# Row normalisation by the absolute sum, fp32: another division of the scaling between VectorE and ScalarE, and one row sum moved in the first tile

## Chip, cores, metric

One core of one Trainium2 chip. The metric is the device time of the whole program in microseconds (us) on that core. A change counts as faster or slower from 2% on.

## The reference

```python
x = np.random.randn(32, 512, 1024).astype(np.float32)

def reference(x):
    sums = np.sum(np.abs(x), axis=-1, keepdims=True)
    return (x / (sums + 1e-8)).astype(np.float32)
```

That is 16384 rows of 1024 elements, 67.1 MB in and 67.1 MB out, with little arithmetic for each byte.

## The kernel before

The rows go through on-chip memory in eleven tiles: ten with 12 rows per partition (128 x 12 x 1024 fp32, 6.29 MB) and a last one with 8 (4.19 MB). There are four tile buffers. SyncE issues the loads, ScalarE's queue the stores, and a load waits until the store that last used its buffer has landed. VectorE forms the sums and reciprocals of a tile and scales most of its rows in place; ScalarE scales the others at the same time.

```python
    R = 12
    BUFS = 4
    HEAD = 32
    ...
    rows = [R] * ((per_partition - HEAD) // R + 2) + [HEAD - 2 * R]   # 10 x 12, then 8
    ...
    def normalize(x_tile, r0, k, kv):          # k rows, VectorE scales the first kv
        s = stats.tile([P, R], FP32)
        nc.vector.tensor_reduce(out=s[:, :k], in_=x_tile[:, r0 : r0 + k, :],
            axis=mybir.AxisListType.X, op=mybir.AluOpType.add, apply_absolute_value=True)
        nc.vector.tensor_scalar_add(out=s[:, :k], in0=s[:, :k], scalar1=EPS)
        inv = stats.tile([P, R], FP32)
        nc.vector.reciprocal(out=inv[:, :k], in_=s[:, :k])
        nc.vector.tensor_mul(...)              # rows 0 .. kv, times inv
        for r in range(kv, k):                 # the other rows on ScalarE
            row = x_tile[:, r0 + r, :]
            nc.scalar.activation(out=row, in_=row,
                func=mybir.ActivationFunctionType.Copy, scale=inv[:, r : r + 1])

    for i, k in enumerate(rows):
        x_tile = sbuf.tile([P, R, d], FP32)
        nc.sync.dma_start(out=x_tile[:, :k, :], in_=piece(x_flat, i))
        normalize(x_tile, 0, k, k - k // 3 - (i == 0))   # 7+5 in tile 0, 8+4, 6+2 in the last
        nc.scalar.dma_start(out=piece(out_flat, i), in_=x_tile[:, :k, :])
```

## Time and profile before

| | before |
|---|---|
| time, median of the first 3 runs | 317.16 us (316.67 to 318.14) |
| profiled span | 315.5 us |
| VectorE busy | 234.7 us |
| ScalarE busy | 47.2 us |
| transfers | 134.2 MB, mean share of the 16 engines 0.99 |
| one tile in the steady stage | 29.0 us, VectorE 22.2 us of it |

The prediction below shows the lines that carry the argument. Three more from the timeline of the kernel before will be needed (start, duration, engine, line, operation; in brackets the idle time just before and what ended it): the issue of the first store, the first instruction of the last tile, and the issue of the last store.

```profile
38.83 0.37 ACTq L81 DMA_DIRECT2D out_dram<-x_tile  x1
...
280.36 8.69 DVE L51 TENSOR_REDUCE s<-x_tile 128x8 f32<-128x8192 f32 x1 [1.96 <-DMA x_tile<-in_x_dram]
...
296.24 0.34 ACTq L81 DMA_DIRECT2D out_dram<-x_tile  x1
```

DMA instructions show only their issue. The data move later: the last store, issued at 296.24, landed 18.2 us after that.

### The profile page before, as it was taken

How to read it: one execution, taken by the hardware profiler on the slowest of the kernel's cores; microseconds unless marked ns; L12 is line 12 of the kernel's file. 1: busy time of each engine (PE TensorE's matmuls, PEld its weight loads, DVE VectorE, ACT ScalarE, POOL GpSimd, SP SyncE). 2: the span in 40 equal slices, each digit the busy share in tenths (PEclk: the TensorE clock that was granted, in tenths of full speed). 3: DMA queues.
4: the chain of work that ended last, by engine and by line, in shares of the span. 5: the costliest groups of instructions: out<-in, count | busy, mean ns of one | idle time of the engine just before them, and what ended most of it. 6: DMA issues, size and time to landing. Idle time of an engine off the chain costs nothing.

```text
span 315.5 us, 206 instructions
## 1 busy us (share of the span) xinstructions
DVE 234.7 (74%) x44; ACT 47.2 (15%) x44; POOL 0.2 (0%) x4
## 2 busy tenths in 40 slices
DVE  0079999999999399929955992899199659979500
ACT  0010603105005001300500050013004000502000
POOL 0000000000000000000000000000000000000000
DMA  8999999999999999999999999999999999999996
GB/s 330 467 399 430 467 343 455 399 467 430 399 467 430 399 486 411 405 486 405 424 474 399 436 461 399 467 430 399 467 425 405 474 403 459 407 472 411 424 432 274
DMA packets 3169, 134.23 MB, mean 425 GB/s; under 512 B 352, under 2 KB 352, under 8 KB 352
## 3 DMA queue, kind: packets, MB, share of 16 engines
q1 hardware_dynamic: 1584, 67.11, 49.8%
q10 hardware_dynamic: 1584, 67.11, 49.1%
q14 instruction: 1, 0.01, 0.0%
HBM read 67.11 MB, written 67.11 MB: 425 GB/s over the span
## 4 chain that ended last, share of the span: by engine, by line
another core or an unknown queue 36%; DMA 31%; DVE 26%; SPq 0%; issue 0%; DVEq 0%; ACTq 0%
DMA x_tile<-in_x_dram 16%; DMA out_dram<-x_tile 15%; DVE s L51 15%; DVE x_tile L61 10%; SPq L78 0%; DVE inv L60 0%; DVE s L58 0%; DVEq L60 0%; ACTq L81 0%
## 5 line engine op out<-in xcount | busy, mean ns | idle before, releaser
L51 DVE TENSOR_REDUCE s<-x_tile 128x12 f32<-128x12288 f32 (+1 forms) x11 | 138.2, 12563 | 59.8 <-DMA x_tile<-in_x_dram 59.8
L61 DVE TENSOR_TENSOR x_tile<-x_tile,inv 128x8192 f32<-128x8192 f32 (+2 forms) x11 | 92.4, 8401 | 0.4
L68 ACT ACTIVATE x_tile<-x_tile,inv 128x1024 f32<-128x1024 f32 x43 | 45.9, 1136 | 226.9 <-DVE inv L60 226.9
L68 ACT ACT_TABLE_LOAD x1 | 1.3, 1283 | 17.7 <-DMA x_tile<-in_x_dram 17.7
L60 DVE RECIPROCAL inv<-s 128x12 f32<-128x12 f32 (+1 forms) x11 | 2.5, 226 | 0.9
L58 DVE TENSOR_SCALAR s<-s 128x12 f32<-128x12 f32 (+1 forms) x11 | 1.9, 173 | 0.4
L96 POOL MEMSET const-bfloat16-1.0<- 128x1 bf16 x1 | 0.1, 102 | 0.0
L96 POOL MEMSET const-uint8-127<- 128x1 uint8 x1 | 0.1, 102 | 0.0
L96 POOL MEMSET const-float32-0.0<- 128x1 f32 x1 | 0.1, 99 | 0.2 <-issue 0.2
L96 POOL MEMSET const-float32-1.0<- 128x1 f32 x1 | 0.1, 99 | 0.0
## 6 DMA issues: line engine op xcount, KB each, us to landing
x_tile<-in_x_dram SPq DMA_DIRECT2D x10, 6144.0 KB, 37.6
out_dram<-x_tile ACTq DMA_DIRECT2D x10, 6144.0 KB, 50.7
x_tile<-in_x_dram SPq DMA_DIRECT2D x1, 4096.0 KB, 32.3
out_dram<-x_tile ACTq DMA_DIRECT2D x1, 4096.0 KB, 18.2
```

The source lines that it names most:

```text
L51: nc.vector.tensor_reduce(out=s[:, :k], in_=x_tile[:, r0 : r0 + k, :], axis=mybir.AxisListType.X, op=mybir.AluOpType.add, apply_absolute_v ...
L58: nc.vector.tensor_scalar_add(out=s[:, :k], in0=s[:, :k], scalar1=EPS)
L60: nc.vector.reciprocal(out=inv[:, :k], in_=s[:, :k])
L61: nc.vector.tensor_mul(out=x_tile[:, r0 : r0 + kv, :], in0=x_tile[:, r0 : r0 + kv, :], in1=inv[:, :kv].unsqueeze(2).to_broadcast([P, kv, d]),)
L68: nc.scalar.activation(out=row, in_=row, func=mybir.ActivationFunctionType.Copy, scale=inv[:, r : r + 1],)
L96: nc = _bacc.Bacc("TRN2", target_bir_lowering=False, num_devices=1)
```

## The change

In the first tile ScalarE forms the sum of one row (an Abs that hands out its sum and writes the values to a scratch tile in PSUM), so that VectorE sums 11 rows; the scaling there stays 7 and 5. In every other tile ScalarE scales two rows only, VectorE the rest: ten of twelve in tiles 1 to 9, six of eight, as before, in the last. The intent as one reads it from the diff: bring the first store forward, and use ScalarE less where VectorE has time.

```diff
+    junk = psum.tile([P, d], FP32)
-    def normalize(x_tile, r0, k, kv):
+    def normalize(x_tile, k, ks, kv):
         nc.vector.tensor_reduce(
-            out=s[:, :k], in_=x_tile[:, r0 : r0 + k, :], ...
+            out=s[:, :ks], in_=x_tile[:, :ks, :], ...
+        for r in range(ks, k):
+            nc.scalar.activation(
+                out=junk[:, :], in_=x_tile[:, r, :],
+                func=mybir.ActivationFunctionType.Abs,
+                accum_out=s[:, r : r + 1],
+            )
 ...
-            normalize(x_tile, 0, k, k - k // 3 - (i == 0))
+            if i == 0:
+                normalize(x_tile, k, k - 1, k - 5)
+            else:
+                normalize(x_tile, k, k, k - 2)
```

More of the change, by code (lines that the diff above doesn't have):

```diff
@@ L46 @@
     stats = ctx.enter_context(tc.tile_pool(name="stats", bufs=4))
-    def normalize(x_tile, r0, k, kv):
+    psum = ctx.enter_context(
+        tc.tile_pool(name="psum", bufs=1, space=bass.MemoryType.PSUM)
+    )
+    junk = psum.tile([P, d], FP32)
+    def normalize(x_tile, k, ks, kv):
         s = stats.tile([P, R], FP32)
         nc.vector.tensor_reduce(
-            out=s[:, :k],
-            in_=x_tile[:, r0 : r0 + k, :],
+            out=s[:, :ks],
+            in_=x_tile[:, :ks, :],
             axis=mybir.AxisListType.X,
@@ L57, in normalize @@
         )
+        for r in range(ks, k):
+            nc.scalar.activation(
+                out=junk[:, :],
+                in_=x_tile[:, r, :],
+                func=mybir.ActivationFunctionType.Abs,
+                accum_out=s[:, r : r + 1],
+            )
         nc.vector.tensor_scalar_add(out=s[:, :k], in0=s[:, :k], scalar1=EPS)
@@ L61, in normalize @@
         nc.vector.tensor_mul(
-            out=x_tile[:, r0 : r0 + kv, :],
-            in0=x_tile[:, r0 : r0 + kv, :],
+            out=x_tile[:, :kv, :],
+            in0=x_tile[:, :kv, :],
             in1=inv[:, :kv].unsqueeze(2).to_broadcast([P, kv, d]),
@@ L66, in normalize @@
         for r in range(kv, k):
-            row = x_tile[:, r0 + r, :]
+            row = x_tile[:, r, :]
             nc.scalar.activation(
```

## The prediction

> **What bounds the kernel now.** I read the page's slices first, because they say whether any engine is full all the time.
>
> ```profile
> span 315.5 us, 206 instructions
> DVE 234.7 (74%) x44; ACT 47.2 (15%) x44; POOL 0.2 (0%) x4
> DVE  0079999999999399929955992899199659979500
> ACT  0010603105005001300500050013004000502000
> DMA  8999999999999999999999999999999999999996
> ```
>
> DVE (VectorE) has holes from the middle on, ACT (ScalarE) is nearly idle, and the DMA row is full from the first slice to the last. The view by stretches gives the same in numbers (stretch, its length, busy time of DVE, ACT and POOL, granted clock, DMA share, GB/s):
>
> ```profile
> 4.00:38.80 34.80, 21.04 (x5) 6.59 (x6) 0.00 (x0) 1.00 1.01 436
> 38.80:111.00 72.20, 65.81 (x12) 12.80 (x12) 0.00 (x0) 1.00 1.01 430
> 111.00:256.00 145.00, 110.24 (x20) 21.32 (x20) 0.00 (x0) 1.00 1.00 433
> 280.30:296.30 16.00, 15.62 (x4) 2.19 (x2) 0.00 (x0) 1.00 0.99 430
> 296.30:315.50 19.20, 0.00 (x0) 0.00 (x0) 0.00 (x0) 1.00 0.83 357
> ```
>
> The rate is the same with loads alone (4 to 38.8), with loads and stores mixed (38.8 to 280), and with stores alone (from 280.3). Only the last stretch is lower, because it holds the end of the transfers. The tensors are 134.2 MB; at 433 GB/s that is 310.0 us, and about 2.5 us of start-up and 3 us of run-out make the 315.5 us span. So the kernel is a transfer of fixed size at a fixed rate. A change of the arithmetic can matter only where it leaves the transfer engines without work.
>
> The third view, the timeline, shows whether it could. Here is one tile of the steady stage, to the start of the next (start, duration, engine, line; in brackets what the engine waited for):
>
> ```profile
> 111.17 12.95 DVE L51 TENSOR_REDUCE s<-x_tile 128x12 f32<-128x12288 f32 x1 [6.26 <-DMA x_tile<-in_x_dram]
> 124.71 4.26 ACT L68 ACTIVATE x_tile<-x_tile,inv 128x1024 f32<-128x1024 f32 x4 [24.21 <-DVE inv L60]
> 124.71 8.69 DVE L61 TENSOR_TENSOR x_tile<-x_tile,inv 128x8192 f32<-128x8192 f32 x1
> 133.49 0.34 ACTq L81 DMA_DIRECT2D out_dram<-x_tile  x1
> 140.20 12.95 DVE L51 TENSOR_REDUCE s<-x_tile 128x12 f32<-128x12288 f32 x1 [6.80 <-DMA x_tile<-in_x_dram]
> ```
>
> A tile comes every 29.0 us (140.20 less 111.17; 2 x 6.29 MB in that time is 434 GB/s). VectorE works 22.3 us of it, then waits 6.8 us for the next load. The scaling is split so that ScalarE ends 4.4 us before VectorE, so VectorE's part sets when the store is issued. Last, the chain of waits (start, duration, what):
>
> ```profile
> 82.95 48.50 DMA out_dram<-x_tile
> 131.52 0.33 SPq L78
> 131.85 28.65 another core or an unknown queue
> 160.63 0.33 SPq L78
> 160.96 28.49 another core or an unknown queue
> 248.08 32.26 DMA x_tile<-in_x_dram
> ```
>
> A load is issued when a store lands and frees its buffer. Stores land at 131.4, 160.5, 189.4, 218.5 and 247.9, one per 29 us: the stores of tiles 2 to 6, in order. Tile 3's store was issued at 105.00 and landed at 160.5, so when tile 4's was issued at 133.49 there were 27 us of the earlier one to go. The store queue is one tile deep in work all the time. The load queue is too: the load issued at 131.85 stands behind one that lands at 140.2.
>
> **What the Trainium skill says.** "DMA: Bandwidth & Descriptors", section "Where 436 GB/s comes from", puts the ceiling of the 16 transfer ports at 435.2 GB/s; the trace agrees, with 430 to 436 in every full stretch. The same section says that the memory side binds at about 358 GB/s per core; the trace does not agree (425 GB/s over the whole span), and the measurement decides. The page's section "Queues, rings and completion order" says that each transfer engine alternates between the queues that have work. That fits 29 us per 6.29 MB store, half of 434 GB/s while both queues are full. "ScalarE: Activation LUTs", section "What ACT_TABLE_LOAD costs", gives an ACTIVATE 186 ns + 0.833 ns per element, and 93 ns for each pointer operand: 1132 ns for 1024 elements with a pointer scale, and the trace has exactly 1132 ns (minimum and median of the 43). Its section "Table sets: the hidden batching unit" says that cheap functions, copy and abs among them, are in every set. So the new Abs should need no second table load; the build of the changed program indeed has one load.
>
> **The change part by part.**
>
> First tile. VectorE sums 11 rows, not 12. The reduces of 12 rows and 8 rows took 12.95 and 8.686 us, so a row costs (12.95 - 8.686)/4 = 1.066 us, and the new reduce takes 11.89 us. The twelfth row goes to ScalarE: the table load, 1.28 us, which was there before too, then one Abs that writes to a scratch tile in PSUM and gives the row sum. I take 1.04 us by the formula above without pointer (an estimate from the skill's page), and some 0.2 us for handing out the sum. ScalarE starts at 17.7, so the sum is there at about 20.3, 9 us before VectorE's ends at 29.55: wholly hidden. The split of the scaling stays 7 and 5 rows. The first store goes out 1.07 us sooner, at about 37.8 and not 38.83. At that time the transfer engines are full of loads (share 1.01, four loads queued), so this brings nothing forward: the same bytes are moved in another order. Gain about 0.
>
> Tiles 1 to 9. VectorE scales ten rows, not eight. Eight rows take 8.69, six 6.56: 1.067 us a row, so ten take 10.83 us, 2.13 more. ScalarE's part falls from 4.26 to 2.19 us (the last tile's two rows show that figure), off the path before and after. VectorE's tile becomes 12.95 + 0.55 for the two small steps and gaps + 10.83 = 24.3 us against a period of 29.0. Its wait for the load shrinks from 6.8 to 4.7 us, and the store is issued 2.1 us later, with 25 us of the earlier store still to go. On the path: 0.
>
> Before the steady stage VectorE runs without waits, so there the delays add up. It starts at 17.66. A tile took 22.06 us there (reduce 38.66 to reduce 60.72), so it will take 24.2. Tile 0 ends at 37.7, tile 1 at about 61.9, tile 2 at 86.1, tile 3 at 110.3. Before, these were 38.7, 60.8, 82.9 and 104.9. Load 4 lands at 111.17, so tile 4 still waits, though only 0.9 us. Tile 3's store goes out 5.4 us later, at 110.4, while tile 2's store lands at about 131: 20 us of cover. On the path: 0.
>
> Last tile. It has eight rows, and k - 2 is six as before. Tile 9's reduce starts at 256.18, so VectorE is through with it at 280.5; the last load lands at 280.34. The last tile is therefore late by about 0.2 us, and its store is issued at about 296.4 and not 296.24. From 296.3 on, 19.2 us x 357 GB/s = 6.85 MB were still moved, of which the last store is 4.19; so 2.66 MB of tile 9's store, or 6.1 us at 433 GB/s, were still ahead of it. The 0.2 us are hidden.
>
> Sums of busy time: DVE 234.7 - 1.07 + 9 x 2.13 = 252.8 us (80%); ACT 47.2 - 9 x 2.07 + 1.2 = 29.8 us (9%). Effect on the time: 0 + 0 + 0, so 317.1 us, as now (runs 316.67 to 318.14).
>
> **The rivals.** (1) VectorE becomes the bound. Against it: 24.3 us of 29.0. By itself its chain would be 17.66 + 20.1 + 9 x 24.3 + 16 for the last tile = 272.5, and with the last store's 18.2 us to landing 290.7, which is below 315.5. (2) The later stores let the store queue run dry, and each tile pays its 2.1 us: up to 9 x 2.1 = 19 us, 336 us. Against it: 20 to 25 us of queued stores at every issue. The 16 engines do not run quite in step and some reach the end of a store before others, but nothing in the shares shows a skew of 20 us. (3) The earlier first store is worth its 1.07 us: 316.1. For it, the first tile is the one place where the author takes work off VectorE; against it, loads alone already ran at 436 GB/s. (4) The last store starts late by the full 2.1 us that tile 9 lost: still within the 6.1 us of cover, so 317.1 too; it would take three times as much to show. (5) VectorE's longer multiplication slows the transfers through the memory they share. In the steady stage the multiply stretches ran at 452 GB/s and the idle ones at 455, so I see no such cost; the reduce stretches showed 427, but reduces don't get longer. If the added 2.1 us per tile ran at 427 instead of 455, that would be 6% of 2.1 us, 0.13 us a tile, 1.2 us in all: 318.3.
>
> **Range and chances.** The mechanism leaves 0, the small rivals -1.1 and +1.2, and the runs of one kernel spread from 316.67 to 318.14. So 317.1 us, and 316.3 to 318.1 should hold it 8 times in 10. A move over 2% (6.3 us) needs rival 2 or something that no view shows: faster 0.01, within 2% 0.97, slower 0.02.
>
> **What would show it.** Each step has its mark in the profile of the changed kernel: reduce of 11 rows near 11.9 us and first store issued near 37.8; multiply of ten rows near 10.83 us; VectorE's waits in the steady stage near 4.7 us with the period still 29.0; reduce of tile 4 still waiting for its load; DMA row full in every slice but the ends, 433 GB/s in the middle; last store issued near 296.4, landing near 314.5. I am wrong if the period is not 29.0 us, if a slice of the DMA row in the middle falls under 9, or if the wait of SyncE for stores moves the loads apart.

## The result, and the profile after

| | before | after |
|---|---|---|
| time, median of 6 runs each, same rounds | 317.32 us (316.67 to 318.14) | 317.74 us (317.17 to 318.03) |
| ratio | | 1.0009, 95% interval 0.9992 to 1.0026 |

The time is the same. A ratio here is formed from the runs of both kernels in the same rounds, so it is not quite the ratio of the medians. Executions over 1.5% slower than the fastest of the same kernel are left out of the means.

The page of the changed kernel, busy times and slices:

```profile
span 315.8 us, 190 instructions
DVE 252.9 (80%) x44; ACT 29.6 (9%) x28; POOL 0.2 (0%) x4
DVE  0079999999999989939994995899399949999600
DMA  8999999999999999999999999999999999999996
```

VectorE gained 18.2 us of work and ScalarE lost 17.6 us, and the DMA row is the same digit for digit. The timeline of the changed kernel at the first tile, in one tile of the steady stage, and at the last tile:

```profile
17.87 1.03 ACT L65 ACTIVATE junk<-x_tile 128x1024 f32<-128x1024 f32 x1 [15.86 <-DMA x_tile<-in_x_dram]
17.87 11.89 DVE L57 TENSOR_REDUCE s<-x_tile 128x11 f32<-128x11264 f32 x1 [17.87 <-DMA x_tile<-in_x_dram]
18.83 0.19 ACT L65 ACTIVATION_READ_ACCUMULATOR junk<-x_tile 128x1 f32 x1
...
38.05 0.38 ACTq L98 DMA_DIRECT2D out_dram<-x_tile  x1
...
198.79 12.95 DVE L57 TENSOR_REDUCE s<-x_tile 128x12 f32<-128x12288 f32 x1 [4.70 <-DMA x_tile<-in_x_dram]
...
212.32 10.82 DVE L74 TENSOR_TENSOR x_tile<-x_tile,inv 128x10240 f32<-128x10240 f32 x1
212.32 2.19 ACT L81 ACTIVATE x_tile<-x_tile,inv 128x1024 f32<-128x1024 f32 x2 [26.87 <-DVE inv L73]
223.24 0.34 ACTq L98 DMA_DIRECT2D out_dram<-x_tile  x1
227.90 12.95 DVE L57 TENSOR_REDUCE s<-x_tile 128x12 f32<-128x12288 f32 x1 [4.75 <-DMA x_tile<-in_x_dram]
...
281.25 8.69 DVE L57 TENSOR_REDUCE s<-x_tile 128x8 f32<-128x8192 f32 x1
...
297.12 0.34 ACTq L98 DMA_DIRECT2D out_dram<-x_tile  x1
```

The sum on ScalarE is over at 19.0 us and VectorE's at 29.8. The first store leaves at 38.05, 0.8 us sooner. A steady tile still takes 29.1 us (227.90 less 198.79); only VectorE's wait for the load has shrunk, from 6.8 to 4.7 us. The last store leaves 0.9 us later. None of this reaches the end.

By stretches (stretch, length, busy time of DVE, ACT and POOL, clock, DMA share, GB/s), the changed kernel:

```profile
111.00:256.00 145.00, 120.90 (x20) 10.94 (x10) 0.00 (x0) 1.00 1.00 433
...
296.30:315.80 19.50, 0.74 (x1) 0.00 (x0) 0.00 (x0) 1.00 0.83 359
```

The rate of the steady stage is 433 GB/s in both kernels, with 10.7 us more of VectorE in the stretch.

One view misleads here, the summary of the chain that ended last. First the kernel before, then the changed one:

```profile
another core or an unknown queue 36%; DMA 31%; DVE 26%; SPq 0%; issue 0%; DVEq 0%; ACTq 0%
```

```profile
DVE 34%; DMA 32%; another core or an unknown queue 27%; SPq 0%; issue 0%; DVEq 0%; ACTq 0%
```

Read alone, it says that VectorE now carries a third of the time. But the chain only follows who released whom, and for the first 110 us it runs through VectorE while the transfer engines beside it are full. The slices and the stretches say what is scarce.

### The profile page after: what moved, and what is told of

Read it like the earlier page. It is cut to its first block, busy times and chain, and to the rows that moved or that the text cites. A ratio compares the mean times of both kernels' runs of the same rounds, so it can differ in the third digit from the quotient of the medians.

```text
span 315.8 us, 190 instructions
## 1 busy us (share of the span) xinstructions
DVE 252.9 (80%) x44; ACT 29.6 (9%) x28; POOL 0.2 (0%) x4
## 4 chain that ended last, share of the span: by engine, by line
DVE 34%; DMA 32%; another core or an unknown queue 27%; SPq 0%; issue 0%; DVEq 0%; ACTq 0%
DVE s L57 19%; DMA x_tile<-in_x_dram 17%; DMA out_dram<-x_tile 15%; DVE x_tile L74 15%; DVE inv L73 0%; SPq L91 0%; DVE s L71 0%; DVEq L73 0%; DVEq L71 0%; ACTq L98 0%
## 5 line engine op out<-in xcount | busy, mean ns | idle before, releaser
L57 DVE TENSOR_REDUCE s<-x_tile 128x12 f32<-128x12288 f32 (+2 forms) x11 | 137.1, 12466 | 42.5 <-DMA x_tile<-in_x_dram 42.4
L74 DVE TENSOR_TENSOR x_tile<-x_tile,inv 128x10240 f32<-128x10240 f32 (+2 forms) x11 | 111.6, 10146 | 0.4
L81 ACT ACTIVATE x_tile<-x_tile,inv 128x1024 f32<-128x1024 f32 x25 | 27.2, 1140 | 246.5 <-DVE inv L73 246.5
L65 ACT ACTIVATE junk<-x_tile 128x1024 f32<-128x1024 f32 x1 | 1.0, 1028 | 15.9 <-DMA x_tile<-in_x_dram 15.9
```

Source lines behind the costliest of these rows:

```text
L57: nc.vector.tensor_reduce(out=s[:, :ks], in_=x_tile[:, :ks, :], axis=mybir.AxisListType.X, op=mybir.AluOpType.add, apply_absolute_value=True,)
L65: nc.scalar.activation(out=junk[:, :], in_=x_tile[:, r, :], func=mybir.ActivationFunctionType.Abs, accum_out=s[:, r : r + 1],)
L74: nc.vector.tensor_mul(out=x_tile[:, :kv, :], in0=x_tile[:, :kv, :], in1=inv[:, :kv].unsqueeze(2).to_broadcast([P, kv, d]),)
L81: nc.scalar.activation(out=row, in_=row, func=mybir.ActivationFunctionType.Copy, scale=inv[:, r : r + 1],)
```

## The experiments

All were run with the kernel before on the same chip, and each compares with that. The theory: 134.2 MB at a fixed rate set the time, and the arithmetic matters only if it leaves the transfer engines without work. Rivals: the two halves of the change cancel; later stores cost; VectorE's work slows the transfers.

### Each half of the change alone

First half only (the changed kernel with the old split in tiles 1 to 10):

```diff
-                normalize(x_tile, k, k, k - 2)
+                normalize(x_tile, k, k, k - k // 3)
```

> Only the first part of the change: ScalarE sums one row of tile 0, all other tiles keep the 8/4 split. Theory (transfers of fixed size at a fixed rate; the arithmetic hides behind them): 317.3 us, within 0.5 of the kernel before, with the first store issued about 0.8 us sooner. Rival (the two parts cancel: the first tile's 1 us is really gained and the new split loses it again): 316.3 us.

Measured: 317.37 us against 316.83, ratio 1.0015 (0.9993 to 1.0037).

Second half only (the kernel before with the new split):

```diff
-            normalize(x_tile, 0, k, k - k // 3 - (i == 0))
+            normalize(x_tile, 0, k, k - 5 if i == 0 else k - 2)
```

> Only the second part: 10/2 split on tiles 1 to 9, tile 0 sums all its rows on VectorE. Theory: 317.3 us, within 0.5 of before. Rival (cancelling): about 318.4, as it carries the loss without the gain. Rival (each tile pays its 2.1 us later store): 336.

Measured: 317.69 us against 316.83, ratio 1.0018 (0.9994 to 1.0042).

A gain of 1 us in the first half would be a ratio of 0.9968, which lies outside its interval, so the halves do not cancel. That the second half costs something cannot be excluded at this resolution, up to 1.3 us by the upper end of its interval; the 19 us of the rival can. A run further below with twice this dose (VectorE scales all rows but tile 0's) narrows it: ratio 1.0001, upper end 1.0023, 0.7 us.

### No arithmetic at all

```diff
-            normalize(x_tile, 0, k, k - k // 3 - (i == 0))
```

> No arithmetic at all (wrong result on purpose): each tile is stored as it was loaded, same tiles, queues and buffers. Theory: 316 to 317.5 us, the floor of the transfers. Rival (the arithmetic, its waits or its memory traffic still cost something between the stages): clearly below, 312 or less.

Measured: 316.62 us against 316.83, ratio 0.9987 (0.9965 to 1.0009). The result is wrong, on purpose. With each tile stored as it came, the program takes as long as with all its arithmetic, though its first store leaves at 17.8 us. This is the floor for these tiles, queues and buffers, and both kernels stand on it: no division of the arithmetic can win anything here.

### Twice the dose: VectorE scales every row

```diff
-            normalize(x_tile, 0, k, k - k // 3 - (i == 0))
+            normalize(x_tile, 0, k, k)
```

> VectorE scales every row, ScalarE none: twice the dose of the new split (4.3 us more per tile of VectorE than before), and the last tile too is 2.1 us later. VectorE needs 26.4 us of the 29.0 us period. Theory: still 317.3 to 317.8 us, because the last store goes out near 302, inside the 6 us that the store ahead of it covers. Rival (VectorE's longer multiply slows the transfers beside it, up to 0.13 us a tile per 2.1 us): about 319.5. Rival (later stores cost): 340 or more.

Measured: 325.35 us (322.32 to 325.45) against 316.83, ratio 1.0226 (1.0184 to 1.0269). My expectation failed by 8 us, and none of the rivals named that figure. In its trace load 9 was there for VectorE at 262.65 us, not at 256.18, and the last store left at 306.9 where I had expected 302; then the engines idled between two stores (DMA share 0.42 from 304 to 308 us).

The trace held a clue that the views by share don't show. Each transfer runs on 16 engines and each engine reports its part, so the trace has 16 landings for each transfer; no view lists them. Here the last came up to 14.5 us after the first; in the kernel before at most 3.0. By the 2% rule this run is "unclear", as its interval contains 1.02; that it is slower than the kernel before is outside the noise. This edit does two things: it makes VectorE's tiles longer, and, as tile 0 has no help either, it moves the first store from 38.8 to 44.3 us. The next two runs take them apart.

### All rows on VectorE, except in tile 0

```diff
-            normalize(x_tile, 0, k, k - k // 3 - (i == 0))
+            normalize(x_tile, 0, k, k - 5 if i == 0 else k)
```

> As e3 (VectorE scales every row), but tile 0 keeps the split of 7 and 5, so that its store goes out near 38.8 us as before. e3 took 325 us and not the 317.5 I expected. In its trace the first store goes out at 44.3, and from then on the 16 transfer engines run out of step: the last of them lands its part of a load up to 14 us after the first, against 3 us in the kernel before. Theory A (the late first store brought the engines out of step): here they stay in step, within 3 us, and the time is 317.5 (last tile ready near 300.5, cover to 302). Theory B (VectorE's slower tiles, 26.4 us, did it): as e3, out of step and 323 to 326.

Measured: 317.03 us against 316.87, ratio 1.0001 (0.9979 to 1.0023).

### All rows on VectorE in tile 0 only

```diff
-            normalize(x_tile, 0, k, k - k // 3 - (i == 0))
+            normalize(x_tile, 0, k, k if i == 0 else k - k // 3)
```

> The kernel before with one edit: VectorE scales all 12 rows of tile 0, so that the first store goes out near 44.2 us; all other tiles keep 8 and 4. Theory A (the late first store brings the engines out of step): the landings spread over 5 us and more as in e3; the time stays near 317 to 320, as VectorE has 6.8 us a tile in hand to absorb late loads. Theory B (the slower tiles did it): in step, 317.2.

Measured: 323.46 us (321.96 to 325.50) against 316.87, ratio 1.0206 (1.0158 to 1.0254). Theory A named the cause rightly and the size wrongly: I had expected at most 320.

The two are opposite to what their doses suggest. Ten tiles with 4.3 us more VectorE work (2.1 in the last) cost nothing, and one tile with 5.4 us more costs 6.6 us. Later stores do not cost by themselves: in the good run stores 2 to 4 left at 91.5, 117.8 and 144.2 us, in the bad one at 88.4, 110.4 and 138.7. It is the first store that is later in the bad run, 44.2 against 38.9 us. The stretch from the first store to the steady stage, first for all rows but tile 0's, then for tile 0 only:

```profile
38.80:111.00 72.20, 71.89 (x12) 0.00 (x0) 0.00 (x0) 1.00 1.01 430
```

```profile
38.80:111.00 72.20, 71.25 (x13) 14.08 (x13) 0.00 (x0) 1.00 1.00 411
```

In the bad run the engines are as busy (share 1.00) but move 411 GB/s, not 430: 72.2 us x 19 GB/s = 1.4 MB less, 3.2 us at 433 GB/s. So in this stretch the engines did not stand idle; they took longer for the same bytes. That is less than half of the 8.0 us by which the span of this run was longer (323.5 against 315.5 us). Most of the rest is idle time at the end, where the landings of the last two stores spread over 8.0 and 6.4 us:

```profile
296.30:323.50 27.20, 8.71 (x4) 2.19 (x2) 0.00 (x0) 1.00 0.74 320
```

Of these 27.2 us 26% were idle, 7.1 us; in the kernel before it was 17% of 19.2 us, 3.3 us (its line stands in the prediction). The queues from 60 to 85 us (packets, MB, share of the engines' time; q1 has the loads, q10 the stores), the kernel before, then the bad run:

```profile
q1 hardware_dynamic: 126, 5.41, 49.9%
q10 hardware_dynamic: 123, 5.26, 48.6%
```

```profile
q10 hardware_dynamic: 158, 6.98, 68.7%
q1 hardware_dynamic: 82, 3.24, 31.8%
```

Before, both queues share the engines evenly. In the bad run loads get 3.2 of 10.2 MB. Part of that has a plain reason. From 40 to 60 us, with the store not yet there, loads had got more than before (5.85 MB against 4.03), so load 3 was through sooner, on its first engine at 75.4 us, and load 4 could be issued only when store 0 had landed on all engines and freed its buffer, at 80.4 us. In between one engine after the other had no load to do. In the kernel before load 4 was issued at 73.5 us, and load 3 landed from 80.3 to 82.2 us.

### The same lateness by another route, less of it, and more of it

Useless reduces on VectorE in tile 0 (into a scratch tile), all splits as before; and the split 10 and 2 in tile 0 (the edit in short; the run hands the list of row counts to `normalize` as an argument):

```diff
# 5 rows more in tile 0  (12 rows: for m in [12])
+        for m in ([5] if i == 0 else []):
+            j = stats.tile([P, R], FP32)
+            nc.vector.tensor_reduce(out=j[:, :m], in_=x_tile[:, r0 : r0 + m, :], ...)
# 10 and 2 in tile 0
-            normalize(x_tile, 0, k, k - k // 3 - (i == 0))
+            normalize(x_tile, 0, k, k - 2 if i == 0 else k - k // 3)
```

> The kernel before with 5.5 us of useless VectorE work (a reduce of 5 rows into a scratch tile) on tile 0 only, all splits kept. The first store goes out near 44.3 us, as in e11, but by another route. Theory A (the time of the first store alone brings the transfer engines out of step): landings spread over 4 us and more, 321 to 325 us as e11. Rival (what mattered in e11 was ScalarE's absence from tile 0): in step and 317.2.

Measured: 322.80 us (321.84 to 324.31) against 316.81, ratio 1.0175 (1.0144 to 1.0207). So it is the lateness of tile 0 and its store (the verdict by the 2% rule is "unclear" here too); ScalarE's part in tile 0 has nothing to do with it.

> The kernel before with tile 0 split 10 and 2, not 7 and 5: the first store goes out near 42.0 us, between the good 38.8 and the bad 44.2. Theory A1 (it must not meet the start of the fourth load, at 46 us when loads run alone, almost at once): 42.0 is 4 us ahead, spread under 3 us, 317 to 318. Theory A2 (every us of lateness costs, about 6.6 us for 5.4 us): about 321.

Measured: 317.06 us against 316.81, ratio 1.0007 (0.9988 to 1.0025). So lateness does not cost in proportion: 42.2 us is as good as 38.8.

> The kernel before with 13.0 us of useless VectorE work on tile 0: the first store goes out near 51.8 us, 5 us after the fourth load began. Theory A1 (only the coincidence of the first store with the start of the fourth load is bad): less spread than e11, 317 to 319. Theory A2 (lateness costs, as the load queue runs out before the first store frees a buffer): worse than e11, 326 or more.

Measured: 322.61, 319.50, 324.69 and 317.17 us against a median of 316.81. The runs scatter over 2.4%, one of them stands on the floor, and the profiled one counts as slow. No run was as bad as A2 asked (326 or more), and not all were as good as A1 asked (317 to 319). Inconclusive.

The spreads of all these runs, from the landings in the traces (time from the first engine's landing to the last's, us; loads and stores are counted from 0; the profiled run of the last row is a slow one):

```
run                            first store   load 3 and store 0   largest later   time
no arithmetic                      17.8          0.7   0.6              0.7       316.6
changed kernel                     38.05         0.6   0.6              1.1       317.7
before                             38.83         1.9   2.5              3.0       317.3
all rows but tile 0's              38.86         1.9   2.6              2.7       317.0
tile 0 split 10 and 2              42.16         0.9   0.6              3.0       317.1
5 rows more in tile 0              44.09         5.5   3.9              8.2       322.8
all rows of tile 0                 44.22         4.8   3.1              8.0       323.5
all rows                           44.34         5.9   4.2             14.5       325.4
12 rows more in tile 0             51.61         2.0   0.8              6.1       317 to 325
```

Three kernels on three chips with a first store at 44.1 to 44.3 us are out of step from the first store on, and all are slow. Those at 42.2 us and earlier are not. What is special at 44 us is open. When loads run alone, as in the last four rows of the table up to the first store, load 2 has landed at about 47 us, and the packets of load 3 begin at 46 us. The packets of store 0 begin at 48.7 us in the three slow kernels, some 3 us after those of load 3. In the run at 42.2 us they begin 3.6 us before them (46.9 and 50.5). So a coincidence is not what tells these runs apart by the packets; the order is. With it goes another mark: in all of the last four rows load 3 has landed on its first engine (67.7 to 75.4 us) before load 4 is issued (77.2 to 80.6 us), so the load queue runs empty; in the other five load 4 is issued in time. Neither is shown to be the cause: at 51.6 us (a slow run's trace) the order is the same and the queue is empty longest, and yet one run of four stood on the floor. Why the engines then take longer for their bytes is not shown by any of these traces either.

### How late the last tile may be

The changed kernel, with useless reduces in the last tile of 4 rows, and of 8 and 4 rows (the edit in short, as above):

```diff
+        for m in ([4] if i == len(rows) - 1 else []):      # or [8, 4]
+            j = stats.tile([P, R], FP32)
+            nc.vector.tensor_reduce(out=j[:, :m], in_=x_tile[:, :m, :], ...)
```

> The changed kernel with 4.4 us of useless VectorE work (a reduce of 4 rows into a scratch tile) added to the last tile only. The last store then goes out 4.4 us later, near 301.5. In the trace of the changed kernel 5.7 us of the earlier store were still to move when the last was issued (7.0 MB after 296.3 us, less 0.36 up to 297.1, less 4.19 of its own, at 433 GB/s). Theory: cover not used up, 317.7 us, at most 0.5 more. Rival (the last tile's chain sets the end directly): 322.

Measured: 317.48 us against 316.87, ratio 1.0030 (0.9995 to 1.0064); the changed kernel itself had 317.74. The last store left at 301.1 us, 4.0 us later, and nothing came of it.

> The same with 13.1 us added to the last tile (reduces of 8 and of 4 rows). Theory: 13.1 less the 5.7 us of cover shows, 7.4 us: 325 us. Rival (all of it shows): 331. Rival (the transfers hide this too): 317.7.

Measured: 324.62 us, ratio 1.0249 (1.0215 to 1.0284). The page's DMA row and the issue of the last store:

```profile
DMA  8999999999999999999999999999999999999456
```

```profile
310.36 0.34 ACTq L107 DMA_DIRECT2D out_dram<-x_tile  x1
```

The store left 13.2 us later than in the changed kernel, and the time grew by 324.62 - 317.74 = 6.9 us, so 6.3 us were covered (5.7 by the estimate). The 317.74 is from other rounds; from the 317.48 of the 4-row run, in the same rounds as this one, it is 7.1 us and 6.1 covered. The rest is the dip to 4 and 5 near the end: the store before had landed at 305.1 us on the last engine, and the engines had nothing to do until this one.

### VectorE near, but below, the period of the transfers

The changed kernel with the 4-row reduce in tiles 1 to 9 (the same loop, with `1 <= i < len(rows) - 1`):

> The changed kernel with a useless reduce of 4 rows (4.4 us) on tiles 1 to 9, none on tile 0 and none on the last, so that the first store stays at 38.0. VectorE then needs 28.6 us a tile, still less than the 29.0 us period of the transfers. Theory A (a VectorE tile below the transfers' period costs nothing): 318 us. Theory B (VectorE's whole chain has to be done by about 303 us): its chain ends at 38.0 + 9 x 28.6 + 15.9 = 311.3 and the last store then needs some 12 us more: 323 us of span, 325 us. Rival (each added us counts): 317.7 + 9 x 4.4 = 357.

Measured: 324.23 us (324.20 to 324.29), ratio 1.0231 (1.0216 to 1.0246). Theory B. By stretches:

```profile
111.00:256.00 145.00, 144.25 (x29) 12.51 (x12) 0.00 (x0) 1.00 1.00 434
...
280.30:296.30 16.00, 15.61 (x5) 2.19 (x2) 0.00 (x0) 1.00 0.57 246
```

VectorE is full, the transfers still run at 434 GB/s up to 280 us, and then they starve (0.57). Here the engines were in step (spread 1.2 us at most). VectorE needed about 28.4 us a tile (reduce at 66.09, the next at 94.48), below the period of 29.0, and still set the end (its last store left at 309.75, 12.6 us later than in the changed kernel), for it starts 18 us late, does tile 0, and must be through with all eleven tiles while something is left to store.

## Why the prediction was right

- **The bound.** A transfer of fixed size at a fixed rate: shown. Without arithmetic the time is the same (316.62), and the rate was 433 GB/s in the steady stage of both kernels.
- **First tile.** Reduce of 11 rows 11.89 us as worked out; Abs 1.03 and its sum 0.19, together 1.2 us as estimated. The first store came 0.8 and not 1.07 us sooner in the profiled runs, because the first load landed at 17.87 and not at 17.66. One thing was not foreseen: the table load moved ahead of the wait for data, to 0.72 us. The worth was 0, as predicted: the first half alone shows no gain.
- **Tiles 1 to 9.** Ten rows took 10.82 us (10.83), the wait shrank to 4.7 (4.7), the period stayed. Tile 4 still waited for its load, 1.0 us (0.9).
- **Last tile.** The store left at 297.1, not 296.4, as load 9 and the reduce that waits for it came 0.6 us later; the predicted cover of 6.1 us was measured as 6.1 to 6.3 and not used up.
- **Sums.** VectorE 252.9 us (252.8), ScalarE 29.6 (29.8).
- **The rivals.** VectorE as the bound: not at 24.3 us a tile, nor at 26.4 with the first store on time; yes at 28.4. So its allowance ends earlier than the comparison with 29.0 us suggests; the other sum in that rival, VectorE's whole chain added up to its end, is the one that counts. VectorE's work slowing the transfers: no; in the runs in step they ran at 431 to 434 GB/s from 111 to 256 us, with VectorE busy for 109 to 144 of these 145 us.
- **Readings that were not quite right.** VectorE works 22.2 us of a steady tile, not 22.3 (133.40 less 111.17). "430 to 436 in every full stretch" leaves out the stretch from 256 to 280.3 us, which ran at 439, above the 435.2 that is called the ceiling; its share of 1.01 says that this view is good to about 1%. The 452 and 455 GB/s of rival 5 come from windows of 7 to 9 us, and one idle window of the same table, at 249.38 us, ran at 431, so they could not have shown a difference of a few GB/s. And the 358 GB/s that the trace is said not to agree with holds, by the skill, when two cores stream (see the closing list).
- **The weakest argument.** "20 to 25 us of queued stores" treats the 16 engines as one. The prediction named their skew and set it aside because the shares show none; but the shares don't show it in the bad runs either. That neither kernel comes near a bad start was not argued for, and in that the prediction was lucky. The experiments show that the start is more delicate than this cover suggests: 5.3 us more before the first store cost 6 us. The changed kernel moves away from that edge by 0.8 us.

## What to carry to other kernels

First find out what the transfers alone take: one run with the arithmetic removed gives the floor and ends the search for gains above it. Where they are the bound, do not compare an engine's tile time with the period; add up its chain from the first landing to the last store, and see what is still queued when that store is issued. Moving work between idle engines was free in the middle here, up to 26.4 us of VectorE in a period of 29.0, but the first and last tile are not the middle: here a first store 3 us late was free, and one 5 us late cost about 2%.

## What the Trainium skill lacked or had wrong

- "DMA: Bandwidth & Descriptors", section "Where 436 GB/s comes from": it lets the memory side bind at about 358 GB/s for transfers between HBM and on-chip memory, without a condition. The condition, that both cores of a memory domain stream, stands in another section of the page, "Measured (HBM→SBUF, 128 partitions, SWDGE, issued from GpSimd)". The one core of this program sustained 430 to 439 GB/s in the full stretches of the kernel before, for loads, for stores and for both, close to the fabric ceiling of 435.2 that the same section gives.
- The same page, section "Why a DMA increments its semaphore by 16 and not by 1", says that the engines of a transfer finish independently, but not how far apart. Here the spread was 0.4 to 3.0 us in good runs and up to 14.5 us in bad ones, which took about 2% longer, and the busy share did not show it (411 GB/s at a share of 1.00).
- "ScalarE: Activation LUTs" mentions the accumulator output of an ACTIVATE without its cost: here a separate instruction of 186 ns after an Abs of 1028 ns over 1024 elements.
- No page says how an engine just below the transfers' period can still set the end: 28.4 us a tile against 29.0 gave 324.2 us in place of 317.7.
